# A two-layer encoder block: the Fourier projection unfolded, with its channels folded on eviction, and layer 1's weights split mostly in the down projection

## The chip, the cores and the metric

The kernel runs on one core of one Trainium2 chip. The metric is the device time of one execution in microseconds, as the median of several runs. Lower is better. One further execution was profiled; every row of the trace that is shown comes from that one.

## What is computed

A trunk of two layers over 512 positions and 1024 channels, all in float32. In each layer the Fourier part, the attention part and a convolutional feed-forward part (FFN) follow one another:

```python
h   = rmsnorm(x, norm1[l])
p   = h @ w_in[l]                       # columns: u (512) | q (8x64) | k (2x64) | v (2x64)
y_f = fft2(u, axes=(positions, channels), norm="ortho").real @ w_fourier[l] + b_fourier[l]
y_a = windowed_gqa(rope(rmsnorm(q)), rope(rmsnorm(k)), v, sink[l])   # |i-j| <= 128
x   = x + concat(rmsnorm(y_f), rmsnorm(y_a)) @ w_o[l]
h   = rmsnorm(x, norm2[l])
up  = dwconv3(h @ w_up[l])              # 1024 -> 2 x 2816
x   = x + (silu(up[:, :2816]) * up[:, 2816:]) @ w_down[l]
```

The real part of a two-dimensional FFT is cos·u·cos − sin·u·sin. Cosine rows are symmetric and sine rows antisymmetric, so each axis of length 512 can be folded: element i and element 512−i are added for the cosine half (indices 0 to 256) and subtracted for the sine half (255 values).

## The kernel before

**Numbers in two pieces.** Every operand of a large matmul is kept as a sum of two values, hi and lo, of a reduced-precision type. `split` and `wsplit` make them: ACT copies the value into hi (line 97 or 123), and DVE, or POOL where that is given, subtracts hi from the value to get lo (line 101 for a scaled source, through the helper `stt` on line 92; otherwise through the helper `tt` on line 89). `mm3` (lines 106 to 108) then issues three matmuls, hi·hi, lo·hi and hi·lo, into one PSUM bank. Since `act`, `tt` and `stt` are helpers, nearly all ACT work is on line 86 of the profile and most of DVE and POOL is on 89 and 92; the tiles tell the groups apart.

**Order of the work.** The kernel is written with a tile framework. It tracks the dependencies, gives out the buffers of each tag, and orders the instructions of each engine by a simulated timeline and by their place in the program, so the order on an engine isn't the order in the text. An engine takes its own instructions strictly in that order. Three things are set by hand: the number of buffers of each tag (`TEMPS`, `BANKS`), `issue_after` in `proj`, which holds the matmuls of the output projection's first half behind numbered steps of the attention, and the generator `presplit`.

**One layer, in the order of the program:**

1. `col_rstd` and `row_rstd` (lines 202 to 216) make the norm's factor `r1` per position down the partitions, and `rb1` along the rows. 
2. q, k and v: two groups (k with one q pair and v, then the other three q pairs), each 8 channel tiles × 4 position blocks × 3 matmuls of 384 columns. The positions are the stationary side (`xg`, tag `act`, 8 buffers).
3. `fold_h` (line 351): for each of the 8 channel tiles, h = x·g·rb1 on DVE, the positions folded (`fold`, line 299: a copy of two columns on DVE, an addition and a subtraction of 255 columns on POOL), and the result split into the tag `slab`.
4. `prep` (line 372) for k and q pair 3 (norm, rotary tables partly on POOL, split), then `turn_k` and `turn_q`, which transpose them on TensorE.
5. The Fourier projection (line 486): the weights' columns are folded too, by `load_wu` on DVE and POOL in layer 0. For each of 8 channel tiles, `mm3` runs on pieces `pee` (3 row pieces of 128, 128 and 1, 258 columns) and `poo` (2 row pieces, 256 columns): 8 × 5 × 3 = 120 matmuls.
6. `prep` for the q pairs 0 to 2, then `attention` for 4 pairs of heads: scores (line 450), a masked minimum on DVE (line 454), exponential on ACT, division on POOL (line 459), transposes on TensorE (line 462), split, and the product with v.
7. `stage_out` (line 515) evicts and splits `pee` and `poo`. Two DFT stages follow (line 526) of 36 matmuls each, against the tables `th` and `tl`, each with its eviction, then the projection with w_fourier (line 561), whose folded rows come in `w_fold` and are added on POOL in layer 0.
8. The output projection w_o in two halves (Fourier, attention), with the next norm's tiles made by `norm_tile` on the way.
9. The FFN in two halves of 11 tiles: 22 up projections (24 matmuls of 512 columns each) and 8 down projections (33 each).

**Layer 1's weights.** During layer 0's FFN `presplit(1)` loads layer 1's w_qkv, w_in, w_fold and w_o, splits them into `tA` tiles (6 buffers), and SyncE's queue stores the pieces in DRAM (`kept`, line 142); layer 1 fetches them with `fetch`. It makes 44 keys. `next(ahead)` makes one, and it stands after each up projection (line 658) and once after each half (line 692), so all are made during the up projections, one per 24 matmuls. Its raw loads use the ring `wraw` (3 buffers), which w_up and w_down use as well.

Of the kernel before, what the change touches and what calls it, by code (L numbers as in the profile page):

```python
# [37 lines left out]
def encoder_kernel(tc, t):  # L38
# [28 lines left out]
    def f(x):  # L67
# [4 lines left out]
    TEMPS = {"act": (1024, 8), "m4": (1024, 5), "slab": (1028, 4), "pT": (2560, 2),  # L72
             "tA": (512, 6), "tF": (512, 6), "sq": (512, 2)}
# [61 lines left out]
    def presplit(l):  # L135

        def keep(key, src):
# [4 lines left out]
            return lambda: [nc.sync.dma_start(o, f(z)) for o, z in zip(kept[key], two)]  # L142

        def store(waiting, w):
            if waiting:
                waiting.pop()()
            if w:
                waiting.append(w)

        late = []  # L150
        for grp in (1, 0):
            for kk in range(KT // 2):
                raw = wload(t["w_qkv"][l, grp, kk], 768)
                for i in range(2):
                    store(late, keep(f"qkv{grp}{2 * kk + i}", raw[:, i * 384:(i + 1) * 384]))
                    yield
        for kk in range(KT // 2):
            raw = wtile()
            nc.sync.dma_start(raw.rearrange("p (k c) -> p k c", k=2),
                              t["w_in"][l, 2 * kk * P:2 * (kk + 1) * P, 0:FW].rearrange("(k p) c -> p k c", p=P))  # L160
            for k in range(2):
                w = temp(512, "tA")
                fold(w, raw[:, k * 512:(k + 1) * 512], nc.vector)
                store(late, keep(f"u{2 * kk + k}", w))
                yield
        for j in range(NF):
            raw = wload(t["w_fold"][l, j], 1024)
            w = temp(512, "tA")
            tt(w[:, :256], raw[:, :256], raw[:, 512:768], ALU.add)
            tt(w[:, 256:], raw[:, 256:512], raw[:, 768:], ALU.subtract)  # L170
            store(late, keep(f"f{j}", w))
            yield
        for half in range(2):
            for mp in range(KT // 2):
                raw = wload(t["w_o"][l, half, :, mp * 1024:(mp + 1) * 1024], 1024)
                for i in range(2):
                    store(late, keep(f"o{half}{2 * mp + i}", raw[:, i * 512:(i + 1) * 512]))
                    yield
        store(late, None)
        while True:  # L180
            yield
# [65 lines left out]
    zero = temp(512, "sq")  # L247
    nc.vector.memset(zero, 0.0)
    warm = temp(512, "sq", F32R)
# [19 lines left out]
    def load_tables():  # L269
        for i in range(2):  # L270
            raw = wload(t["dft"][i], 512)
            th = cp.tile([P, 512], F32R, tag=f"th{i}", name=f"th{i}")
            tl = cp.tile([P, 512], F32R, tag=f"tl{i}", name=f"tl{i}")
            split(th, tl, raw)
            tab.append((th, tl))
        alt = wtile()[:1, :258]
# [4 lines left out]
    def add_square(acc, src, first, eng=nc.gpsimd, tag="sq"):  # L281
# [17 lines left out]
    def fold(dst, src, eng):  # L299

        nc.vector.tensor_copy(dst[..., 0:257:256], src[..., 0:257:256])
        tt(dst[..., 1:256], src[..., 1:256], src[..., 511:256:-1], ALU.add, eng)
        tt(dst[..., 257:512], src[..., 1:256], src[..., 511:256:-1], ALU.subtract, eng)

    def load_wu(l, kk):

        raw = wtile()
        nc.sync.dma_start(raw.rearrange("p (k c) -> p k c", k=2),
                          t["w_in"][l, 2 * kk * P:2 * (kk + 1) * P, 0:FW].rearrange("(k p) c -> p k c", p=P))
        out = []  # L310
        for k in range(2):
            w = temp(512, "tA")
            fold(w, raw[:, k * 512:(k + 1) * 512], nc.gpsimd)
            out.append(w)
        return out
# [4 lines left out]
    for l in range(L):  # L320

        r1 = col_rstd(acc, 1.0 / D)
        rb1 = row_rstd(r1)
        qraw = {}
        for grp in (1, 0):
            pq = [psum("mm" if b < 3 else "av") for b in range(NB)]
# [22 lines left out]
        hs = {}  # L349

        def fold_h(k, eng):
            hr = temp(512, "tF")
            hf = temp(512, "tF")
            stt(hr, x[k], g1[:, l, k:k + 1], rb1, ALU.mult, ALU.mult)
            fold(hf, hr, eng)
            hs[k] = pair("slab")
            split(hs[k][:, 0, :], hs[k][:, 1, :], hf)

        for k in range(4):
            fold_h(k, nc.gpsimd)  # L360
# [11 lines left out]
        def prep(us):  # L372
# [4 lines left out]
            for i, u in enumerate(us):  # L377
                two = temp(1024, "act").rearrange("p (z b h d) -> p z b h d", z=2, **dims)
# [99 lines left out]

        if l == 0:
            load_tables()  # L480

# [3 lines left out]

        pee = [psum(), psum(), psum("av")]
        poo = psum()
        for kk in range(KT // 2):
            if not l:
                wu = load_wu(l, kk)  # L490
            for k in (2 * kk, 2 * kk + 1):
                if k not in hs:
                    fold_h(k, nc.gpsimd)
                w = fetch(f"u{k}") if l else wsplit(wu[k % 2])
                h = hs[k]
                st, sp_ = k == 0, k == KT - 1
                we = [z[:, 0:258] for z in w]
                wo = [z[:, 256:512] for z in w]
                for m, (c0, c1) in enumerate(((0, 128), (128, 256), (256, 257))):
                    mm3(pee[m][:c1 - c0, :258], [h[:, s, c0:c1] for s in range(2)], we, st, sp_)  # L500
                mm3(poo[:, 0:256], [h[:, s, 257:385] for s in range(2)], wo, st, sp_, skip_group_check=True)
                mm3(poo[:127, 256:512], [h[:, s, 385:512] for s in range(2)], wo, False, sp_, skip_group_check=True)
# [7 lines left out]
        def tail_out(pe, scale):  # L510
            b = tp.tile([1, 2, 258], F32R, tag="tail", name=nm("tail"), bufs=2)
# [3 lines left out]
        def stage_out(pe, po, scale):  # L515
            tiles = []
            for m in range(2):
                a = pair("slab", 514)
                n = P - m
                split(a[:, 0, :258], a[:, 1, :258], pe[m][:, :258], scale=scale)  # L520
                split(a[:n, 0, 258:514], a[:n, 1, 258:514], po[:n, m * 256:(m + 1) * 256], scale=scale)
                tiles.append(a)
            return tiles, tail_out(pe, scale)

        ue, ut = stage_out(pee, poo, 1.0)
        for stage in range(2):
            pe = [psum() for _ in range(2)]
            po = psum()
            pe.append(psum())
            for m, (c0, c1) in enumerate(((0, 128), (128, 256), (256, 257))):  # L530
                o = pe[m][:c1 - c0, :258]
                for i in range(2):
                    u2 = [ue[i][:, s, :] for s in range(2)]
                    if stage == 0:
                        mm3(o, [z[:, c0:c1] for z in u2], [z[:, 0:258] for z in tab[i]], i == 0, False)
                    else:
                        mm3(o, [z[:, c0:c1] for z in tab[i]], [z[:, 0:258] for z in u2], i == 0, False)
# [244 lines left out]
```

## Time and profile before

| | |
|---|---|
| median of 3 runs | 1111.37 us (1110.5 to 1114.45) |
| the profiled execution, its own time | 1112.89 us |
| its span from first to last instruction | 1111.1 us |
| mean granted TensorE clock over the span | 0.988 |
| layer 0 up to the last matmul of the second norm | 0 to 227.1 us |
| layer 0's FFN | 226.9 to 573.2 us |
| layer 1 up to the same place | 579.8 to 766.1 us |
| layer 1's FFN | 765.9 to 1111.1 us |

In rows that group instructions, the columns are: line, engine, operation, output tile <- input tiles, shape, x count | busy time in us, mean ns of one | idle time of the engine just before them, and what ended it. In rows of windows: the window, its length, and for each engine busy us (x instructions), then the granted clock of TensorE (PEclk), the share of the DMA engines' time and GB/s. PE is TensorE's matmuls, PEld its weight loads. A matmul's duration overlaps its neighbours', so the pace of a dense stretch is read from the length of the stretch and the number of matmuls in it.

### The profile page before, as it was taken

To read this page: it belongs to the slowest core of one execution; us is meant where nothing else is said; L and a number is where in the kernel's file an instruction comes from. 1 tells how busy PE (TensorE), PEld (TensorE's weight loads), DVE (VectorE), ACT (ScalarE), POOL (GpSimd) and SP (SyncE) were. 2 spreads that over 40 slices of the span, in tenths; PEclk is the share of its full clock that TensorE was granted. 3 is DMA by queue.
4 is the path that set the end of the run, shared out by engine and by line. 5 is a ranking of instruction groups with operands and counts; after the bars stand their busy time and mean duration, and the time that the engine had idled before them with its cause. 6 is when DMAs were issued, how large, how long until landed. Compare 5 with 4: busy or idle time off the path is not lost.

```text
span 1111.1 us, 14836 instructions
## 1 busy us (share of the span) xinstructions
PE 1068.9 (96%) x5187; PEld 892.3 (80%) x5187; DVE 778.9 (70%) x1406; ACT 514.5 (46%) x964; POOL 278.1 (25%) x326
## 2 busy tenths in 40 slices
PE   7878899999999999999999899999999999999998
PEld 6776788788888888778889787878888888888887
DVE  8997874988883477887437968477878535787732
ACT  4536763565552244554412676245555323544421
POOL 5678654511010001111105344050201000010100
PEclk9978999999999999999999999999999999999999
DMA  6312113366643576763355510523232333333241
GB/s 218 110 58 95 39 39 119 122 215 229 207 147 93 196 249 232 231 218 105 87 168 174 188 58 20 171 76 95 95 97 82 104 97 97 112 89 101 78 130 59
DMA packets 58574, 141.65 MB, mean 127 GB/s; under 512 B 6521, under 2 KB 19074, under 8 KB 58498
## 3 DMA queue, kind: packets, MB, share of 16 engines
q1 hardware_dynamic: 58498, 140.69, 40.0%
q8 instruction: 41, 0.67, 0.2%
q14 instruction: 35, 0.29, 0.1%
HBM read 117.60 MB, written 23.07 MB: 127 GB/s over the span
## 4 chain that ended last, share of the span: by engine, by line
PE 72%; DVE 15%; DMA 6%; issue 3%; ACT 2%; POOL 1%; SPq 0%; DVEq 0%; POOLq 0%; ACTq 0%
PE ps L106 22%; PE ps L108 22%; PE ps L107 22%; DVE wlo L89 4%; DMA wraw<-in_w_o_dram 3%; DMA wraw<-in_w_fold_dram 2%; DVE tF L92 2%; DVE act L89 1%; DVE act L92 1%; PE ps L450 1%; PE ps L462 1%; DVE tA L89 1%; DVE tF L89 1%; DVE slab L89 1%; DMA wraw<-in_w_in_dram 1%
## 5 line engine op out<-in xcount | busy, mean ns | idle before, releaser
L89 DVE TENSOR_TENSOR wlo<-wraw,whi 128x512 fp32r<-128x512 f32 (+1 forms) x288 | 234.6, 816 | 113.8 <-ACT whi L86 111.8
L107 PE MATMUL ps<-act,wlo 128*128 128x512 f32 x768 | 300.4, 392 | 3.7 <-DVE wlo L89 3.6
L108 PE MATMUL ps<-act,whi 128*128 128x512 f32 x768 | 300.2, 391 | 3.2 <-DVE act L92 3.1
L86 ACT ACTIVATE whi<-wraw 128x512 fp32r<-128x512 f32 (+1 forms) x300 | 183.5, 613 | 256.1 <-PE ps L108 231.7
L106 PE MATMUL ps<-act,whi 128*128 128x512 f32 x768 | 299.7, 390 | 0.0
L89 POOL TENSOR_TENSOR tF<-tF,tF 128x512 f32<-128x512 f32 x44 | 61.0, 1387 | 535.9 <-DVE tF L92 492.4
L107 PEld LDWEIGHTS ps<-act,wlo 128*128 128x128 f32 x768 | 144.6, 188 | 36.2 <-DVE wlo L89 6.2
L108 PEld LDWEIGHTS ps<-act,whi 128*128 128x128 f32 x768 | 144.6, 188 | 35.5 <-DVE act L92 6.1
L106 PEld LDWEIGHTS ps<-act,whi 128*128 128x128 f32 x768 | 144.5, 188 | 30.2
L92 DVE SCALAR_TENSOR_TENSOR tF<-tF,pb,tF 128x511 f32<-128x511 f32 x176 | 132.8, 759 | 8.7 <-ACT tF L86 5.5
L89 DVE TENSOR_TENSOR tF<-ps,rb 128x512 f32<-128x512 f32 x104 | 70.6, 686 | 43.8 <-PE ps L108 32.6
L106 PE MATMUL ps<-slab,whi 128*128 128x512 f32 (+2 forms) x228 | 87.3, 383 | 1.0 <-ACT slab L86 1.0
L107 PE MATMUL ps<-slab,wlo 128*128 128x512 f32 (+2 forms) x228 | 85.2, 374 | 0.0
L108 PE MATMUL ps<-slab,whi 128*128 128x512 f32 (+2 forms) x228 | 84.9, 375 | 0.1
L86 ACT ACTIVATE tF<-tF,pb 128x512 f32<-128x512 f32 x88 | 71.5, 815 | 15.7 <-DVE tF L89 12.3
L89 DVE TENSOR_TENSOR x<-x,ps 128x512 f32<-128x512 f32 (+1 forms) x49 | 33.0, 676 | 46.1 <-PE ps L108 46.1
L89 POOL TENSOR_TENSOR acc<-acc,sq 128x512 f32<-128x512 f32 x28 | 43.0, 1535 | 60.0 <-ACT sq L86 59.3
L107 PE MATMUL ps<-pT,wlo 128*128 128x512 f32 (+1 forms) x132 | 51.0, 386 | 0.0
L108 PE MATMUL ps<-pT,whi 128*128 128x512 f32 (+1 forms) x132 | 50.8, 385 | 0.0
L106 PE MATMUL ps<-pT,whi 128*128 128x512 f32 (+1 forms) x132 | 50.8, 385 | 0.0
L106 PEld LDWEIGHTS ps<-slab,whi 128*128 128x128 f32 x228 | 42.9, 188 | 8.8 <-ACT slab L86 1.4
L108 PEld LDWEIGHTS ps<-slab,whi 128*128 128x128 f32 x228 | 42.8, 188 | 8.5 <-DVE slab L89 0.4
(171 smaller groups left out, 1791.3 us busy)
## 6 DMA issues: line engine op xcount, KB each, us to landing
wraw<-in_w_up_dram SPq DMA_DIRECT2D x88, 512.0 KB, 3.8
wraw<-in_w_down_dram SPq DMA_DIRECT2D x32, 512.0 KB, 3.5
kept<-tA SPq DMA_DIRECT2D x56, 256.0 KB, 4.3
wraw<-in_w_o_dram SPq DMA_DIRECT2D x16, 512.0 KB, 3.6
whi<-kept SPq DMA_DIRECT2D x28, 256.0 KB, 3.5
wlo<-kept SPq DMA_DIRECT2D x28, 256.0 KB, 3.7
wraw<-in_w_qkv_dram SPq DMA_DIRECT2D x16, 384.0 KB, 3.5
kept<-tA SPq DMA_DIRECT2D x32, 192.0 KB, 2.1
```

The costliest lines, as they stand in the source:

```text
L86: return nc.scalar.activation(out, in_, func, **kw)
L89: return (eng or nc.vector).tensor_tensor(out, a, b, op=op)
L92: return nc.vector.scalar_tensor_tensor(out=out, in0=a, scalar=s, in1=b, op0=op0, op1=op1)
L106: nc.tensor.matmul(out, a[0], b[0], start=start, stop=False, **kw)
L107: nc.tensor.matmul(out, a[1], b[0], start=False, stop=False, **kw)
L108: nc.tensor.matmul(out, a[0], b[1], start=False, stop=stop, **kw)
L450: nc.tensor.matmul(sc[:, :n], qT[p][:, e, i * P:(i + 1) * P], kT[g][:, s, j0 * P:(j1 + 1) * P], start=s == 0, stop=s == 1)
L462: tr = nc.tensor.transpose(pp[:, j * P:(j + 1) * P], pr[:, j * P:(j + 1) * P], ident)
```

## The change

The Fourier projection takes the same stationary tiles `xg` as q, k and v, and the unfolded weights. The result comes out with positions down the partitions and 512 channels along the columns, one PSUM bank for each of the 4 position blocks. On eviction it is scaled by `r1` and its channels are folded. `fold_h`, `rb1` and the folding of w_in are gone. The position axis is no longer folded before the first DFT stage: that stage contracts over 4 blocks of 128 positions, with two more table tiles, made from the first two by alternating signs on ACT. It now stands in front of `prep`.

```diff
 TEMPS:  "slab" (1028, 4) -> (1024, 4);  "tA" (512, 6) -> (512, 5);  "sq" (512, 2) is gone (its users take "tF")
-        rb1 = row_rstd(r1)
-            pq = [psum("mm" if b < 3 else "av") for b in range(NB)]
+            pq = [psum(("mm", "mm", "mm", "av")[b] if grp else ("sc", "sc", "tp", "tp")[b]) for b in range(NB)]
...
-        def fold_h(k, eng):
...
-        for k in range(4):
-            fold_h(k, nc.gpsimd)
+        if l == 0:
+            load_tables()
+        pu = [psum("mm" if b < 3 else "av") for b in range(NB)]
+        for kk in range(KT // 2):
+            raw = None if l else load_wu(l, kk)
+            for k in (2 * kk, 2 * kk + 1):
+                w = fetch(f"u{k}") if l else wsplit(raw[:, (k % 2) * 512:(k % 2 + 1) * 512])
+                for b in range(NB):
+                    mm3(pu[b], [xg[k][:, s, b * P:(b + 1) * P] for s in range(2)], w, k == 0, k == KT - 1)
+        ub = []
+        for b in range(NB):
+            uf = temp(512, "tF")
+            fold(uf, pu[b], r1[:, b:b + 1])
+            a = pair("act")
+            split(a[:, 0, :], a[:, 1, :], uf)
+            ub.append(a)
...
+    def fold(dst, src, scale):
+        up = temp(256, "tF")
+        act(up[:, :255], src[:, 257:512], scale=scale)
+        nc.vector.tensor_scalar(dst[:, 0:257:256], src[:, 0:257:256], scale, None, op0=ALU.mult)
+        stt(dst[:, 1:256], src[:, 1:256], scale, up[:, 254::-1], ALU.mult, ALU.add)
+        stt(dst[:, 257:512], src[:, 1:256], scale, up[:, 254::-1], ALU.mult, ALU.subtract)
...
-                two = temp(1024, "act")...          # in prep
+                two = temp(1024, "slab")...
...
-        pee = [psum(), psum(), psum("av")]          # the folded projection, 120 matmuls
...
+        for m, (c0, c1) in enumerate(((0, 128), (128, 256), (256, 257))):      # first DFT stage
+            for b in range(NB):
+                mm3(pe[m][:c1 - c0, :258], [ub[b][:, s, c0:c1] for s in range(2)], [z[:, 0:258] for z in tab[b]],
+                    b == 0, b == NB - 1)
+        for m in range(2):
+            for b in range(NB):
+                mm3(po[:, m * 256:(m + 1) * 256], [ub[b][:, s, 256 + m * P:384 + m * P] for s in range(2)],
+                    [z[:, 256:512] for z in tab[b]], m == 0 and b == 0, b == NB - 1, skip_group_check=True)
```

The second stage keeps its 36 matmuls. The folded rows of w_fourier are now loaded without the part that repeats (`load_wf`: 2 × 256 of 1024 columns), and `fold_w` makes sum and difference on DVE. `wsplit` of them in layer 0 is on DVE and no longer on POOL, and the squares of the Fourier output are added up on DVE.

`presplit` becomes a list of jobs. The raw tile comes from the tag `m4` (5 buffers), no longer from `wraw`, and it is loaded one job ahead:

```diff
         def keep(key, src):
             two = [temp(n, "tA", F32R) for _ in range(2)]
             split(two[0], two[1], src)
...
+            store()
+            late.append(lambda: [nc.sync.dma_start(o, f(z)) for o, z in zip(kept[key], two)])
...
+        got = jobs[0][0]()
+        for n, (_, keys) in enumerate(jobs):
+            for i, key in enumerate(keys):
+                keep(key, fold_w(got[i]) if key[0] == "f" else got[i])
+                if i == len(keys) - 1 and n + 1 < len(jobs):
+                    got = jobs[n + 1][0]()
+                yield
...
-                    next(ahead)                       # after each up projection
+                    if (2 * n + z) % 3 == 2:
+                        next(ahead)
...
-                tt(ys_[0], ys_[0], ys_[1], ALU.mult, nc.gpsimd)
+                tt(ys_[0], ys_[0], ys_[1], ALU.mult, nc.gpsimd if l else nc.vector)
...
             for m in range(KT):                       # down projection
+                next(ahead)
+                next(ahead)
```

That is 7 keys in the up projections of a half and 16 in its down projections. The key's `u` jobs no longer fold.

More of the change, by code (lines that the diff above doesn't have):

```diff
@@ L141, in keep, with store @@
             kept[key] = [dp.tile([P, n], F32, tag=f"{key}{s}", name=nm("kept")) for s in range(2)]
[L142 to L150, printed above, removed]
+            store()
+            late.append(lambda: [nc.sync.dma_start(o, f(z)) for o, z in zip(kept[key], two)])
+        def store():
+            while late:
+                late.pop()()
@@ L161, in presplit @@
[L161 to L165, printed above, removed]
-        for j in range(NF):
[L167 to L172, printed above, removed]
+            jobs.append((lambda kk=kk: wu(kk), [f"u{2 * kk + i}" for i in range(2)]))
@@ new lines, in encoder_kernel @@
+        ue, ut = stage_out(pe, po, 1.0)
+        pe = [psum(), psum()]
+        po = psum()
+        pe.append(psum())
+        for m, (c0, c1) in enumerate(((0, 128), (128, 256), (256, 257))):
+            o = pe[m][:c1 - c0, :258]
+            for i in range(2):
+                mm3(o, [z[:, c0:c1] for z in tab[i]], [ue[i][:, s, 0:258] for s in range(2)], i == 0, False)
+            for s in range(2):
+                nc.tensor.matmul(o, altr[:, c0:c1], ut[:, s, :], start=False, stop=s == 1)
@@ L691, in encoder_kernel @@
                     nxt.append(norm_tile(m, g1[:, l + 1, :], acc))
-            next(ahead)
             xg = nxt
```

178 lines of the change are left out of this document (70 added, 108 removed).

## The prediction

> **What bounds the kernel now.** I read the page first, for the engines and the slices, then the windows by stage, then the groups of instructions in the one window that looked wrong, then the waits.
>
> ```profile
> PE 1068.9 (96%) x5187; PEld 892.3 (80%) x5187; DVE 778.9 (70%) x1406; ACT 514.5 (46%) x964; POOL 278.1 (25%) x326
> ...
> PE   7878899999999999999999899999999999999998
> ...
> PEclk9978999999999999999999999999999999999999
> ```
>
> TensorE carries the span. Added columns cost time wherever PE is at 9, and a gain must come from the few slices where it isn't: the second to fifth, where PEclk dips too, one near the middle of layer 0's FFN, and around the norms. The windows put sizes on them (layer 0's stretch from 32 to 90; dense FFN; layer 0's and layer 1's FFN; dense folded projection; dense q projection; attention and output part of layer 0 and layer 1).
>
> ```profile
> 32.00:90.00 58.00, 44.95 (x251) 39.01 (x249) 55.48 (x95) 24.71 (x50) 44.38 (x51) 0.83 0.25 75
> 800.00:900.00 100.00, 100.00 (x439) 82.21 (x438) 66.60 (x88) 42.23 (x64) 9.03 (x7) 1.00 0.31 93
> 226.00:573.00 347.00, 343.32 (x1501) 280.47 (x1501) 239.45 (x371) 162.23 (x267) 41.99 (x34) 1.00 0.57 181
> 766.00:1100.00 334.00, 334.00 (x1465) 274.51 (x1464) 218.84 (x292) 141.41 (x214) 28.79 (x22) 1.00 0.32 97
> 624.00:629.20 5.20, 5.20 (x46) 4.88 (x45) 4.54 (x6) 0.37 (x1) 4.57 (x5) 1.00 0.79 244
> 594.00:604.00 10.00, 9.96 (x58) 9.64 (x57) 9.90 (x16) 2.43 (x4) 7.16 (x9) 1.00 0.23 63
> 82.00:178.00 96.00, 87.74 (x529) 73.92 (x530) 71.52 (x207) 64.46 (x164) 61.93 (x92) 0.96 0.17 56
> 630.00:717.00 87.00, 83.72 (x507) 70.44 (x508) 61.74 (x198) 52.38 (x144) 28.51 (x64) 1.00 0.24 78
> ```
>
> These rows give the pace of a matmul at full clock. 512 columns: 100/439 = 0.228 us. 384 columns: 10/58 = 0.172, say 0.174, since one record in the count began earlier. 256 or 258 columns: records there last about 0.28 us, so those counted began within 5.48 us, and 5.48/46 = 0.119.
>
> In 32 to 90 DVE is busy 55.5 of 58 us and POOL 44.4, while PE stands idle for 13 us and runs at a mean clock of 0.83. DVE sets that stretch.
>
> **What fills DVE there, and what goes.** Groups of DVE, POOL and PE in that window, and then two DVE groups in layer 1 (606 to 717), where POOL is mostly idle:
>
> ```profile
> L92 DVE SCALAR_TENSOR_TENSOR tF<-x,pa,rb 128x512 f32<-128x512 f32 x8 | 8.6, 1079 | 0.1
> L89 DVE TENSOR_TENSOR slab<-tF,slab 128x512 fp32r<-128x512 f32 x8 | 7.6, 975 | 0.0
> L89 DVE TENSOR_TENSOR wlo<-tA,whi 128x512 fp32r<-128x512 f32 x8 | 7.1, 887 | 0.0
> L301 DVE COPY tF<-tF 128x2 f32<-128x2 f32 x8 | 4.0, 496 | 0.0
> L301 DVE COPY tA<-wraw 128x2 f32<-128x2 f32 x8 | 3.1, 425 | 0.0
> L92 DVE SCALAR_TENSOR_TENSOR slab<-ps,slab 128x258 fp32r<-128x258 f32 (+2 forms) x6 | 2.3, 410 | 0.1
> L92 DVE SCALAR_TENSOR_TENSOR qk2q<-qk2q,qk2v 128x16 f32<-128x16 f32 x3 | 1.8, 594 | 0.0
> L89 POOL TENSOR_TENSOR tF<-tF 128x255 f32<-128x255 f32 x16 | 15.1, 966 | 14.8 <-DVE tF L92 14.8
> L89 POOL TENSOR_TENSOR tA<-wraw 128x255 f32<-128x255 f32 x16 | 14.3, 923 | 0.5 <-DMA wraw<-in_w_in_dram 0.5
> L107 PE MATMUL ps<-whi,slab 128*128 128x258 f32 (+3 forms) x40 | 12.9, 354 | 3.6 <-DVE slab L89 3.6
> L108 PE MATMUL ps<-wlo,act 128*128 128x384 f32 x31 | 10.6, 346 | 1.3 <-DVE wlo L89 1.3
> ```
> ```profile
> L89 DVE TENSOR_TENSOR slab<-tF,slab 128x512 fp32r<-128x512 f32 x8 | 5.3, 684 | 0.1
> L92 DVE SCALAR_TENSOR_TENSOR qk2q<-qk2q,qk2v 128x16 f32<-128x16 f32 x3 | 0.5, 176 | 0.1
> ```
>
> (Of ACT, for below:)
>
> ```profile
> L86 ACT ACTIVATE slab<-tF 128x512 fp32r<-128x512 f32 x8 | 4.9, 622 | 7.6 <-PE ps L108 4.5 <-POOL tF L89 2.1 <-POOL wraw L89 1.0
> L86 ACT ACTIVATE slab<-ps 128x258 fp32r<-128x258 f32 (+2 forms) x6 | 2.2, 381 | 12.6 <-PE ps L108 10.8 <-PE ps L540 1.5 <-DVE slab L92 0.3
> ```
>
> The change takes `fold_h` and the weight fold out: on DVE 8.6 + 7.6 + 4.0 + 3.1 = 23.3 us, on POOL 15.1 + 14.3 = 29.4 of its 44.4 us. The second effect is as large as it is hidden: a DVE instruction of 16 columns takes 594 ns here and 176 in layer 1, and a 512-column subtraction 975 against 684, because POOL is working beside them. With POOL two thirds empty, the 24 small steps of the two q and k norms, of which the group shown is the slowest, shrink by about half of its 0.42 us on the mean, 24 × 0.2 = 5 us, and the 8 weight splits by 8 × 0.2 = 1.6 us.
>
> New on DVE are four folds on eviction. From the rows: a step of about 256 columns out of PSUM costs 0.41 us, with two of them per block, the two-column scaling lies between 0.18 and 0.5 (I take 0.2), and the subtraction for lo is 0.68. That is 4 × 1.7 = 6.8 us. DVE's load becomes 55.5 − 23.3 − 6.6 + 6.8 = 32 us.
>
> **Part 1, layer 0 from 32 to 90.** PE's own work now, at the paces above: 91 matmuls of 384 columns (the shown 31 and two groups of 30), 15.8 us; 120 of the folded projection, 14.3; the 40 others (transposes and first DFT matmuls) at about 0.115, 4.6. Sum 34.7 us in 58. The change makes the 120 matmuls into 8 × 4 × 3 = 96 of 512 columns, 96 × 0.228 = 21.9, so +7.6. The first DFT stage has (3 + 2) × 4 × 3 = 60 matmuls for 36: 24 × 0.119 = +2.9. `row_rstd` of `rb1` goes; this piece of the chain has its price:
>
> ```profile
> 586.96 0.89 PE ps L213 x8
> ```
>
> So PE has 9.6 us more per layer, and 44.3 us here. With DVE at 32 us, PE becomes the bound, and the projection needs nothing from the q and k preparation, so it covers it: 22 us of matmuls, in which DVE has 5.6 us of weight splits to do. I take 46 us for the stretch, 1.7 above PE's work, for the first folds. **−12.0 us.** The end at 44.3 is one bound, −13.7. The other is that the chain fold, split, DFT isn't covered: one block's fold in sequence (ACT 0.4 and 0.6, DVE 1.7) four times is 11 us at worst, −2.7. I stay near the first, because the transposes of k and q and the first scores are ready by then and need no `ub`.
>
> **Part 2, layer 0's attention and output.** Between 82 and 178 PE is idle for 8.3 us, in layer 1's same part (630 to 717) for 3.3. The difference, 5, is DVE's lateness and POOL's rotary work; I take back 1.5, since the folded w_fourier rows come to DVE: 8 additions of 256 columns and 4 splits, 8 × 0.41 + 4 × 0.69 = 6 us, less one `stage_out` of 4 × 0.41 plus the tail. **−1.5 us.**
>
> **Part 3, layer 1.** No cold clock here. PE waits, from the waits of TensorE between 586 and 640:
>
> ```profile
> PE ps L414 <- DVE m L89: 2.3, 1, 2.3
> PE ps L106 <- DVE vz L92: 1.1, 1, 1.1
> PE ps L425 <- ACT m L86: 0.6, 1, 0.6
> ```
>
> All three wait for preparation on ACT or DVE that would now lie under 22 us of projection matmuls: −4.0, and with a few tenths of fetch waits −4.5. The added 9.6 stays. **+5.1 us.** The bounds are +9.6 (nothing recovered) and +4.
>
> **Part 4, layer 0's FFN.** 1501 matmuls in 347 us, at layer 1's pace (334/1465 = 0.228) 342.2: 4.8 us are lost, 3.7 of them idle. The waits between 370 and 500 and one piece of the chain show the reason:
>
> ```profile
> ACT tA L86 <- DMA wraw<-in_w_o_dram: 19.0, 8, 3.2
> DVE tA L89 <- DMA wraw<-in_w_fold_dram: 9.9, 4, 3.4
> ```
> ```profile
> 377.00 5.59 DMA wraw<-in_w_fold_dram
> ```
>
> ACT and DVE stand in front of a raw tile that was loaded just before it is used, because `wraw` is shared with w_up; the FFN's own splits queue behind on the same engine. With rows of their own and a job's lead, the load is hidden by the preceding job. The keys move to the down projections, where each output has 33 × 0.228 = 7.5 us of matmuls. Costs of DVE per output there, from the groups of the whole run and the DMA issues:
>
> ```profile
> L89 DVE TENSOR_TENSOR wlo<-wraw,whi 128x512 fp32r<-128x512 f32 x240 | 200.2, 834 | 79.3 <-ACT whi L86 77.7
> L89 DVE TENSOR_TENSOR x<-x,ps 128x512 f32<-128x512 f32 x47 | 32.2, 687 | 39.4 <-PE ps L108 39.4
> L92 DVE SCALAR_TENSOR_TENSOR act<-x,pa,act 128x512 fp32r<-128x512 f32 x32 | 32.1, 1008 | 4.1 <-ACT act L86 3.7
> kept<-tA SPq DMA_DIRECT2D x56, 256.0 KB, 4.3
> ```
>
> Three weight splits 2.5, the addition 0.7, two keys 1.4, and in the second half the norm 1.0: 5.6 us at most, under 7.5. The gated product that comes from POOL to DVE (22 × 0.69 us) falls in the up projections, which lose two thirds of their keys. **−4.5 us.** Bounds: −4.8, and above zero for the first rival.
>
> **Sum.** −12.0 − 1.5 + 5.1 − 4.5 = −12.9. The profiled execution took 1112.89 us (1111.1 of span and 1.8 around it), so 1100.0; it lies 1.5 above the median of the runs shown, 1111.37, so I forecast 1098.5. A measurement of this kernel tells about 0.5% from no change: 5.6 us, so faster is below 1105.8 and slower above 1116.9.
>
> **A rule against it.** PE's clock after a wait, in two windows: the wait for `slab`, and what came behind it.
>
> ```profile
> 67.60:71.20 3.60, 0.04 (x1) 0.00 (x0) 3.60 (x7) 1.84 (x4) 2.81 (x3) 0.92 0.21 85
> 71.20:77.80 6.60, 6.56 (x32) 6.01 (x33) 6.50 (x12) 0.00 (x0) 5.28 (x8) 0.53 0.00 0
> ```
>
> A wait of 3.6 us was followed by 6.6 us at 0.53 of the clock, which cost 6.6 × 0.47 = 3.1 us more. The Trainium skill ("TensorE: Matmul & The Clock Gate", part 1, the clock gate) has the clock halved after one idle window of about 3.4 us and full again after one busy window of that length. By that rule an uncovered fold would cost its wait and about 1.7 us; the trace says nearly twice that. The rows decide, and it enters one rival.
>
> **Rivals.**
> *Stores stall the down projections (slower).* Each key takes two of now five `tA` buffers, two keys come back to back, and a store lands 4.3 us after its issue. A key's stores are issued only after the next key's split, and the key after that already needs one of its buffers. If DVE stands for one landing per output, 5.6 + 4.3 = 9.9 us against 7.5, with 2.4 lost, and without the norm 1.4: 8 × 2.4 + 8 × 1.4 = 30 us. It decides once the stall exceeds 1.9 us in the second half. The time: 1098.5 + 4.5 + 30 − 4 (banks that run ahead) = 1129. Against it: the keys of one output and of the next lie 7.5 us apart, longer than a landing, and DVE's order can put the FFN's own splits first.
> *The wait moves (no change).* The folds aren't covered, in both layers: 11 − 1.7 = 9 us in layer 0, some 5 in layer 1, and 3.1 of cold clock after the first: 1098.5 + 17 = 1115. For it: all four banks finish together, at the last channel tile, and ACT has its own queue of evictions.
> *TensorE packs closer (faster still).* DVE freed in both layers lets attention start earlier; PE's idle time of 3.3 us in layer 1's attention and 5 us in layer 0's goes too, with some switching loss: 1098.5 − 10 = 1088.
> That the change does nothing can be excluded: the matmul counts differ.
>
> **Chances.** Forecast 0.57 (1092 to 1105, with a tenth of it above the line), packing 0.15, moved wait 0.18 (a third of it each way of the lines, mostly inside), stores 0.10. Faster: 0.52 + 0.15 = 0.67. The same: 0.05 + 0.11 = 0.16. Slower: 0.10 + 0.07 = 0.17. The range runs from 1088 to 1115: it takes in the packing and most of the moved wait and leaves out the stores.
>
> **What would show it.** In the changed profile, 96 matmuls of 512 columns from `act` directly behind the q projection, without idle time over 1 us; PEclk at 1.0 from 32 to 90; the small DVE steps of `qk2q` under 250 ns; layer 0's output projection done some 13 us earlier than now; layer 1 from its first norm to the second 5 us longer; layer 0's FFN within 343 us with no wait for a raw tile. I am wrong if PE waits over 3 us for `ub`, if DVE waits for `kept` in the down projections, or if layer 1 grows by over 10 us.

## The result, and the profile after

The changed kernel took 1129.91 us (median of 4 runs, 1129.04 to 1130.74) and the kernel before 1112.05 beside it. The ratio is 1.0159, 95% interval 1.0137 to 1.018: slower by 1.6%, where 1098.5 was forecast and the range ended at 1115. The profiled execution took 1129.04 us, with a span of 1127.3 and a mean granted clock of 0.976.

The page of the kernel after, in the lines shown of before:

```profile
PE 1083.1 (96%) x5171; PEld 915.4 (81%) x5171; DVE 749.2 (66%) x1396; ACT 520.5 (46%) x960; POOL 177.8 (16%) x239
...
PE   8989869999999999999999997799999999999998
...
PEclk9989969999999999999999998799999999999999
```

A slice is 28.2 us. DVE and POOL lost 30 and 100 us of work, as the change says, and the weak slice 23 of before (611 to 639 us, in layer 1) is full. But PE has new holes: slice 6 (141 to 169 us) and slices 25 and 26 (676 to 733), all with a low clock. They lie where the two layers have attention and the first half of w_o. The windows of the kernel after show how deep they are:

```profile
32.00:90.00 58.00, 53.00 (x301) 48.04 (x300) 49.07 (x116) 33.64 (x75) 16.94 (x19) 0.94 0.30 98
231.80:573.20 341.40, 341.40 (x1512) 282.82 (x1511) 242.41 (x371) 168.77 (x265) 9.54 (x11) 1.00 0.53 177
130.00:190.00 60.00, 46.58 (x205) 39.29 (x203) 29.77 (x81) 23.16 (x49) 16.29 (x16) 0.80 0.27 88
651.00:741.00 90.00, 75.71 (x411) 64.84 (x410) 50.60 (x170) 39.44 (x108) 20.03 (x52) 0.89 0.21 65
```

The kernel before, in the same stages (in layer 1 its attention and the first half of w_o are over at 717):

```profile
130.00:190.00 60.00, 57.48 (x319) 49.32 (x320) 38.42 (x116) 33.62 (x82) 29.54 (x47) 1.00 0.18 54
651.00:717.00 66.00, 64.94 (x377) 54.62 (x377) 45.27 (x144) 35.96 (x98) 21.53 (x49) 1.00 0.28 88
```

From 130 to 190 the changed kernel issues 205 matmuls for 319, at a clock of 0.80 for 1.00, and no other engine is near full. Nothing is saturated: something waits. Split at the first matmul of layer 1's q, k and v (573.1 us before; the 579.8 of the earlier table is the norm's matmuls, which come a little later):

| us | layer 0 | layer 1 | span |
|---|---|---|---|
| before | 573.1 | 538.0 | 1111.1 |
| forecast (−18.0, +5.1) | 555.1 | 543.1 | 1098.2 |
| after | 573.2 | 554.1 | 1127.3 |

So layer 0's whole gain is missing, and layer 1 lost 16 instead of 5. TensorE's waits of the kernel after between 60 and 240 us (total, times, longest):

```profile
PE ps L106 <- ACT act L86: 5.0, 1, 5.0
PE ps L106 <- ACT tF L86: 4.3, 1, 4.3
PE ps L208 <- DVE accF L89: 3.7, 1, 3.7
PE ps L496 <- DVE pT L89: 3.3, 4, 1.9
PE ps L215 <- DVE nr L92: 2.5, 1, 2.5
```

The first is the wait for `ub`, the first DFT stage's operand. The second, third and fifth are a chain: Fourier output, its squares, its norm. Before, this chain lay among attention's steps. ScalarE's timeline shows when it starts (start, us, engine, line, operation, out <- in). The kernel before:

```profile
107.25 0.48 ACT L86 ACTIVATE tF<-ps,pa 128x258 f32<-128x258 f32 x1 [0.59 <-PE ps L108]
...
121.38 0.46 ACT L86 ACTIVATE tF<-ps,pa 128x258 f32<-128x258 f32 x1
...
129.00 0.69 ACT L86 ACTIVATE act<-ps,pa 128x512 fp32r<-128x512 f32 x1
```

The kernel after:

```profile
121.51 0.59 ACT L86 ACTIVATE tF<-ps 128x512 f32<-128x512 f32 x1
...
140.82 0.67 ACT L86 ACTIVATE act<-ps,pa 128x512 fp32r<-128x512 f32 x1
...
143.76 0.58 ACT L86 ACTIVATE tF<-ps 128x512 f32<-128x512 f32 x1
144.24 0.47 ACT L86 ACTIVATE tF<-ps,pa 128x258 f32<-128x258 f32 x1
```

`tF<-ps,pa` of 258 columns is the eviction of one Fourier output tile (`u`), `act<-ps,pa` closes a pair of heads, and `tF<-ps` is the square of that pair's output. Before, all four evictions were done before the first pair closed. After, the first one comes right behind the last pair's square, at 144 us. With the norm behind it, the first 96 matmuls of w_o, which would fill attention's pauses, all run in one piece behind it (before, they are spread from 140 to 178 us):

```profile
167.00:190.00 23.00, 22.70 (x96) 18.17 (x97) 8.45 (x14) 6.34 (x12) 8.98 (x7) 0.99 0.24 69
```

### The profile page after: what moved, and what is told of

It reads as the page before. It is cut to its first block, busy times and chain, and to the rows that moved or that the text cites. A ratio compares the mean times of both kernels' runs of the same rounds, so it can differ in the third digit from the quotient of the medians.

```text
span 1127.3 us, 14774 instructions
## 1 busy us (share of the span) xinstructions
PE 1083.1 (96%) x5171; PEld 915.4 (81%) x5171; DVE 749.2 (66%) x1396; ACT 520.5 (46%) x960; POOL 177.8 (16%) x239
## 4 chain that ended last, share of the span: by engine, by line
PE 87%; DVE 6%; ACT 2%; issue 2%; DMA 1%; POOL 1%; SPq 0%; DVEq 0%; ACTq 0%
PE ps L106 28%; PE ps L108 28%; PE ps L107 27%; PE ps L484 1%; DVE tA L488 1%; PE ps L496 1%; PE ps L208 1%; DVE wlo L89 1%; DVE pT L89 1%; ACT tA L86 1%; DVE act L92 1%; DMA kept<-tA 1%; DVE tF L92 1%; PE ps L215 1%; DVE x L89 1%
## 5 line engine op out<-in xcount | busy, mean ns | idle before, releaser
L86 ACT ACTIVATE whi<-wraw 128x512 fp32r<-128x512 f32 (+1 forms) x308 | 189.2, 617 | 315.3 <-PE ps L108 278.5
L89 DVE TENSOR_TENSOR wlo<-wraw,whi 128x512 fp32r<-128x512 f32 (+1 forms) x300 | 228.3, 762 | 90.6 <-ACT whi L86 88.8
L106 PE MATMUL ps<-slab,whi 128*128 128x512 f32 (+2 forms) x228 | 88.4, 389 | 7.9 <-ACT tF L86 6.8
L89 POOL TENSOR_TENSOR acc<-acc,tF 128x512 f32<-128x512 f32 x28 | 39.7, 1417 | 352.2 <-ACT tF L86 350.3
L108 PE MATMUL ps<-slab,whi 128*128 128x512 f32 (+2 forms) x228 | 87.0, 384 | 0.3 <-DVE slab L89 0.3
L89 POOL TENSOR_TENSOR tF<-tF,tF 128x512 f32<-128x512 f32 x22 | 30.5, 1386 | 270.4 <-DVE tF L92 229.2
L108 PE MATMUL ps<-wlo,act 128*128 128x384 f32 (+1 forms) x192 | 68.2, 358 | 1.5 <-DVE wlo L89 1.5
L107 PE MATMUL ps<-whi,act 128*128 128x384 f32 (+1 forms) x192 | 68.8, 358 | 0.8 <-DVE act L92 0.8
L106 PE MATMUL ps<-whi,act 128*128 128x384 f32 (+1 forms) x192 | 67.9, 356 | 0.0
L106 PEld LDWEIGHTS ps<-slab,whi 128*128 128x128 f32 x228 | 45.4, 199 | 17.3 <-ACT tF L86 7.2
L108 PEld LDWEIGHTS ps<-slab,whi 128*128 128x128 f32 x228 | 45.3, 199 | 8.8 <-DVE slab L89 1.2
```

The costliest lines, as they stand in the source:

```text
L86: return nc.scalar.activation(out, in_, func, **kw)
L89: return (eng or nc.vector).tensor_tensor(out, a, b, op=op)
L106: nc.tensor.matmul(out, a[0], b[0], start=start, stop=False, **kw)
L107: nc.tensor.matmul(out, a[1], b[0], start=False, stop=False, **kw)
L108: nc.tensor.matmul(out, a[0], b[1], start=False, stop=stop, **kw)
```

## The experiments

**Theory A**: the tag `sq` is gone and its users take `tF`, so attention's squares and the Fourier output now draw on one tag. The framework gives a tag's tiles out in the order of the program's text, and attention stands first there, so the Fourier output must wait until attention has taken its last tile. **The rivals** in the expectations look elsewhere. B is the added TensorE work and the later first DFT stage, which would make the Fourier chain late whatever the tags; C is the count, too few `tF` tiles for all their users. The kernel before took 1112.05 to 1113.47 us (median) beside these runs. All kernels compute the whole reference.

| run | us | ratio to before, 95% interval |
|---|---|---|
| after, squares on `tA` | 1110.18 | 0.998 (0.9966 to 0.9995) |
| before, squares on `tF` | 1150.28 | 1.0336 (1.0312 to 1.036) |
| before, new spread of the split alone | 1108.39 | 0.9958 (0.994 to 0.9976) |
| after, 5 `tF` and 1 `sq` | 1096.95 | 0.9849 (0.9819 to 0.988) |
| before, 8 `tF`, no `sq` | 1152.6 | 1.0343 (1.0325 to 1.0362) |
| 5 + 1, rows on GpSimd | 1095.71 | 0.9842 (0.982 to 0.9864) |
| 5 + 1, rows held back | 1087.36 | 0.9761 (0.9745 to 0.9777) |
| after, attention later in the text | 1094.46 | 0.9826 (0.9806 to 0.9846) |
| after, attention later and rows held back | 1084.15 | 0.9725 (0.9701 to 0.9749) |
| rows held back, old spread of the split | 1087.97 | 0.9766 (0.9742 to 0.979) |
| before, squares on `tF`, attention later | 1113.19 | 0.9991 (0.9974 to 1.0009) |
| the 1084.15 version, `slab` of 1028 | 1090.02 | 0.9792 (0.9774 to 0.981) |

### Which tag the squares use

In the changed kernel, another tag for attention's squares:

```diff
-    add_square(accA, ...)                 # the helper's default tag, here "tF"
+    add_square(accA, ..., tag="tA")
```

> The changed kernel with one edit: the squares of the attention output take a tile of the tag tA and no longer one of tF. Theory A (tiles of one tag are given out in the program's order, so the Fourier output's eviction, which asks for a tF tile later in the program than the attention's squares, had to wait for the last pair of heads, and w_o's first half lost its cover): the Fourier output is evicted among the attention steps, the idle stretches around 130 to 167 and 684 to 718 us shrink by 25 to 33 us together, 1097 to 1105 us. Theory B (the extra TensorE work and the later first DFT stage leave the Fourier chain too late whatever the buffers): 1122 us or more. Theory C (too few tF tiles, their count and not their order): 1122 or more, since tF keeps 6 tiles with three users fewer; a gain of at most 5.

It took 1110.18, 20 less than the changed kernel, where theory A had 25 to 33. The mechanism holds and the price is off; `tA` also holds attention's probabilities, which may be why, but no run shows it. TensorE's waits between 60 and 240 us are now

```profile
PE ps L106 <- ACT act L86: 4.9, 1, 4.9
PE ps L484 <- DVE nmax L488: 4.4, 4, 2.0
```

and the chain of the Fourier output is gone from them. Line 484 is the scores, which wait for the masked minimum on DVE.

The reverse, in the kernel before: its one edit gives it the shared tag and leaves all else.

```diff
-    add_square(accA, ...)                 # the helper's default tag, here "sq"
+    add_square(accA, ..., tag="tF")
```

> The kernel before with that one edit alone the other way: the squares of the attention output take tF tiles in place of their own tag. Nothing else is changed. Theory A: slower by 15 to 30 us, 1127 to 1142, with the Fourier output's evictions after the last pair of heads and w_o's first half in one uncovered piece. Theory B: within 3 us of 1112, since its TensorE work is that of before. Theory C: within 5 us.

1150.28: the shared tag alone costs this kernel 37 us, more than expected. That speaks against theory B, since this kernel has none of the added TensorE work. In the changed kernel, a tile of its own for the squares, taken from `tF`:

```diff
-    "tF": (512, 6)
+    "tF": (512, 5), "sq": (512, 1)
...
-    add_square(accA, ...)
+    add_square(accA, ..., tag="sq")
```

> The changed kernel with one tF tile fewer (5) and that tile as a tag of its own for the squares of the attention output. The total number of tiles is that of the changed kernel. Theory A: the order of giving out is what matters, so about as fast as with the squares on tA, 1097 to 1108 us. Theory C (the number of tF tiles): slower than the changed kernel, over 1130.

1096.95: 33 us less than the changed kernel, with fewer `tF` tiles and the same bytes. That speaks against the count. From 130 to 190 us PE is full again:

```profile
130.00:190.00 60.00, 58.70 (x302) 49.08 (x302) 42.11 (x96) 32.85 (x74) 31.62 (x37) 1.00 0.36 118
```

### Order or number of the tiles

The kernel before with more `tF` tiles and all of its bytes:

```diff
-    "tF": (512, 6), "sq": (512, 2)
+    "tF": (512, 8)
...
-    def add_square(acc, src, first, eng=nc.gpsimd, tag="sq"):
+    def add_square(acc, src, first, eng=nc.gpsimd, tag="tF"):
```

So the squares of the two norms of x are on `tF` here too, and not only attention's.

> The kernel before with its two `sq` tiles made into two more `tF` tiles (8 tF, no sq); everything else as before, so the fold of h and of the weights stays on VectorE. Theory A (tiles of one tag are given out in program order, so the Fourier output's evictions wait for the last of attention's squares, however many tiles there are as long as they are fewer than attention's 16 squares): 1135 to 1155, near the 1150.28 that the shared tag gave with six tiles; the w_o matmuls of the first half stand in one piece behind attention. Theory C (too few tiles, not their order): with as many bytes as before the time is back at 1112 plus or minus 6.

1152.6, as with six tiles. (The expectation's figure of 16 attention squares is wrong: the trace has three that need a tile in a layer.) Eight tiles would hold those three and the first Fourier tiles side by side, and still ScalarE's timeline has the Fourier output behind the last square:

```profile
154.34 0.60 ACT L86 ACTIVATE tF<-ps 128x512 f32<-128x512 f32 x1 [0.82 <-DVE act L92]
154.84 0.84 ACT L86 ACTIVATE tF<-ps,pa 128x258 f32<-128x258 f32 x2
```

So it is the order. If the order is that of the text, moving the text must be enough. The changed kernel with six shared tiles and three lines moved:

```diff
-        attention(3, True)
-        for p in range(3):
-            attention(p, False)
...
             yf.append(y)
+        attention(3, True)
+        for p in range(3):
+            attention(p, False)
         rbF = row_rstd(...)
```

> The changed kernel with its one tag of six `tF` tiles, but with the calls of attention moved behind the Fourier output in the program's text; the issue order by cost stays the scheduler's. Theory A (order of the tag's tiles by program text): the Fourier output's evictions now hold their tiles before attention's squares, overlap is back, 1094 to 1110, with the w_o matmuls spread over attention. If it isn't the order of the tiles but their count, 1122 or more, as the changed kernel's 1129.9. A risk under theory A: now attention's first squares wait for the Fourier output's tiles, and with them attention's probabilities; then 1105 to 1120.

1094.46, 35 us less than the changed kernel, without a byte or an instruction more. In ScalarE's timeline the squares now stand behind the Fourier output:

```profile
103.64 0.48 ACT L86 ACTIVATE tF<-ps,pa 128x258 f32<-128x258 f32 x1 [0.18 <-PE ps L108]
...
118.37 0.48 ACT L86 ACTIVATE tF<-ps,pa 128x258 f32<-128x258 f32 x1 [0.69 <-PE ps L108]
...
129.82 0.60 ACT L86 ACTIVATE tF<-ps 128x512 f32<-128x512 f32 x1
```

The same three lines moved in the kernel before with its squares on `tF`:

> The kernel before with attention's squares on the shared tag `tF` (1150.28 with attention first in the text) and the calls of attention moved behind the Fourier output. Theory A (the tag's tiles are given out in program order): the 38 us go, 1104 to 1118. If the shared tag costs by its number of tiles or in another way, 1130 or more.

1113.19, from 1150.28: level with the kernel before. Theory A is shown from both sides: the shared tag costs 37 us in the kernel before and 33 to 35 in the changed one, and the order of the text takes it away in both. Neither does it alone: with a tag of their own for the squares, attention can stand first in the text at no such cost (1112 and 1096.95).

### The split's spread alone

The kernel before with the new job list, its tiles and its place in the down projections, and none of the projection's change:

```diff
+                if i == len(keys) - 1 and n + 1 < len(jobs):
+                    got = jobs[n + 1][0]()
...
-                    next(ahead)
+                    if (2 * (fi - f0) + z) % 3 == 2:
+                        next(ahead)
...
+                next(ahead)
+                next(ahead)
```

> The kernel before with the new splitting of layer 1's weights alone (raw tiles from m4, one job ahead, 7 keys in the up and 16 in the down projections of a half; u and f keys still folded on DVE). Forecast: layer 0's FFN 4 to 6 us shorter, 1106 to 1108 us. The rival of the prediction (stores stall the down projections): 1120 or more.

1108.39, a ratio of 0.9958: at the slow edge of the forecast, and with no stall. Its FFN of layer 0 takes 342.4 us, from 347.0, without a gap on PE:

```profile
227.50:569.90 342.40, 342.40 (x1506) 282.04 (x1505) 254.52 (x369) 167.61 (x264) 38.71 (x34) 1.00 0.53 180
```

That window opens at the norm's last matmuls, and how many of the FFN's matmuls come before these differs from kernel to kernel. A stretch of equal work is the last 1056 matmuls, from the first down projection of the first half to layer 1: 247.3 us before, 241.7 here, 239.4 in the changed kernel. The run changes the raw tiles' lead and the place of the keys at once, and doesn't tell which of them is worth the 5.5 us.

In the changed kernel the waits of DVE and ACT in the FFN of layer 0 (231 to 574) show what the store rival had feared, and that it doesn't reach PE, which has not one wait there:

```profile
DVE tA L89 <- DMA kept<-tA: 7.4, 4, 3.1
```
```profile
ACT tA L86 <- DMA m<-in_w_o_dram: 8.7, 5, 3.0
```

Is the new spread still worth it where the folds are gone? The version with the rows held back (below), with the old spread (its raw tiles come from `wraw` again):

```diff
...
-                    if (2 * n + z) % 3 == 2:
-                        next(ahead)
+                    next(ahead)
...
-                next(ahead)
-                next(ahead)
...
```

> The version with the rows held back (1087.36) with layer 1's weights split as in the kernel before: one step behind each tile of the gate stage, none in the down projections, the stores one step later, the raw rows in the tile `wraw`. The new spread alone took 3.7 to 4.6 us off the kernel before. If it is worth as much here: 1091 to 1093. If the folds that are gone from the split (eight folded input-weight tiles less) made the old spread harmless: 1087 to 1089.

1087.97 against 1087.36, intervals on top of each other; those 1056 matmuls take 240.3 us, against 239.4. So the spread and the rest of the change in this FFN lead to the same few us and don't add. That rest is two things which no run separates: the folds of w_in are out of the split, and the gated product is on DVE and no longer on POOL.

### The wait of 5 us behind the projection

ScalarE's timeline in the kernel after, before that wait ends at 74.5 us:

```profile
67.81 0.63 ACT L86 ACTIVATE whi<-wraw 128x512 fp32r<-128x512 f32 x1 [6.85 <-DVE wraw L338]
71.57 0.63 ACT L86 ACTIVATE whi<-wraw 128x512 fp32r<-128x512 f32 x1 [3.12 <-DVE wraw L338]
72.10 1.18 ACT L86 ACTIVATE tF<-ps,nr 128x255 f32<-128x255 f32 x3
```

`tF<-ps,nr` is the fold's eviction of the projection. In the run with the rows held back (below) ScalarE takes the first at 67.04 us, so that its bank was ready then; but ScalarE takes its instructions in order, and ahead of it stand high copies of w_fourier rows, each waiting for `fold_w` on DVE (line 338). First, in the five-plus-one version, these folds and low halves on GpSimd:

```diff
-            w = ... wsplit(fold_w(load_wf(l, j)))
+            w = ... wsplit(fold_w(load_wf(l, j), nc.gpsimd), nc.gpsimd)
```

> The five-plus-one version (1096.95) with layer 0's fold of the w_fourier rows and their low halves on GpSimd instead of VectorE. The wait of 5 us for `act` behind the projection is put down to ScalarE, which holds the four high copies of these rows, each waiting for VectorE's fold, ahead of the projection's evictions. If VectorE's queue is what makes these copies late, the wait shrinks to 1 to 3 us and the time is 1093 to 1096. If GpSimd is as late with them as VectorE was (it is slower on such tiles), 1097 to 1100. If the copies aren't the cause, the wait stays at 5 us and the time at 1097.

The wait went from 5.2 to 4.3 us and the time by 1.2, inside the intervals: neither of the first two cases, and inconclusive by itself. Then the rows behind the folds:

```diff
-            split(a[:, 0, :], a[:, 1, :], uf)
+            hi = act(a[:, 0, :], uf)
+            lo = tt(a[:, 1, :], uf, f(a[:, 0, :]), ALU.subtract)
...
-            w = fetch(f"f{j}") if l else wsplit(fold_w(load_wf(l, j)))
+            if l:
+                w = fetch(f"f{j}")
+            else:
+                with tc.issue_after(hi.ins), tc.issue_after(lo.ins):
+                    w = wsplit(fold_w(load_wf(l, j)))
```

> The five-plus-one version (1096.95) with layer 0's fold and split of the w_fourier rows put behind the last fold's eviction in the order of ScalarE and VectorE. If the four high copies ahead of the evictions make the wait of 5 us and the cold clock behind it (7.3 us lost from 68.8 to 80 us), both go: TensorE goes from the projection to the second DFT stage in under 1.5 us, the granted clock stays at 1.0 from 60 to 80 us, and the time is 1089 to 1092. If the evictions themselves are what is late, the wait stays and the time is 1097 or more, since the rows now come later.

1087.36, 9.6 less, a little more than expected. ScalarE takes the first eviction at 67.04 us, and the window from 60 to 80 loses its hole. The five-plus-one version:

```profile
60.00:80.00 20.00, 14.84 (x75) 12.67 (x74) 19.70 (x37) 8.11 (x16) 11.19 (x11) 0.83 0.41 132
```

With the rows held back:

```profile
60.00:80.00 20.00, 19.62 (x122) 16.41 (x122) 18.25 (x41) 11.29 (x24) 7.84 (x8) 1.00 0.10 27
```

Both cures together (attention later in the text, rows held back):

> Six `tF` tiles with attention's calls later in the text (1094.46), and the rows of w_fourier held back as in the run that did this (1096.95 to 1087.36, 9.6 less). If the two gains are of different stretches (the fold at 60 to 80 us, attention from 100 us on), they add: 1085, 1083 to 1088. If the later rows now delay what attention covers, 1088 to 1094.

1084.15, ratio 0.9725 (0.9701 to 0.9749): the gains add, and this beats both kernels. Its page:

```profile
PE 1064.2 (98%) x5171; PEld 899.1 (83%) x5171; DVE 753.2 (70%) x1396; ACT 517.1 (48%) x960; POOL 184.6 (17%) x239
...
PEclk9999999999999999999999999999999999999999
```

### One number: the columns of `slab`

The matmuls of the same FFN code in layer 1 followed each other 0.7% closer in every kernel that had `slab` at 1024 columns. The best version with only this:

```diff
-    "slab": (1024, 4)
+    "slab": (1028, 4)
```

> The best version (1084.15) with one number changed: the tag `slab` gets back its 1028 columns (tiles of 1028 instead of 1024 values; no instruction and no order changes). In every kernel so far with 1028 the first 400 matmuls behind the last norm take 90.8 us and the 400 after them, down projections whose moving side lies in `slab`, 92.0; in every kernel with 1024 both take 90.7 to 90.8. If the place of the `slab` tiles sets this pace, the second 400 take 92.0 again and the time is 1088 to 1090 (2.2 us for each of the two FFNs by these kernels, and up to 1 for the output projections). If the pace comes with the fold of h or anything else that those kernels share, it stays at 90.8 and the time at 1084.

1090.02 (ratio 0.9792, 0.9774 to 0.981, against 0.9725), spans 1087.3 and 1082.7: 4.6 us more by the spans, 5.9 by the medians. The second 400 matmuls behind the last norm take 91.9 us and not 90.7. Groups of TensorE between 860 and 925 us, with mean ns behind the comma. With 1024:

```profile
L106 PE MATMUL ps<-act,whi 128*128 128x512 f32 x38 | 14.8, 389 | 0.0
...
L106 PE MATMUL ps<-slab,whi 128*128 128x512 f32 x20 | 7.8, 389 | 0.0
L106 PE MATMUL ps<-m,whi 128*128 128x512 f32 x18 | 7.0, 389 | 0.0
```

With 1028:

```profile
L106 PE MATMUL ps<-act,whi 128*128 128x512 f32 x33 | 12.8, 389 | 0.0
...
L106 PE MATMUL ps<-slab,whi 128*128 128x512 f32 x20 | 7.9, 393 | 0.0
L106 PE MATMUL ps<-m,whi 128*128 128x512 f32 x18 | 7.1, 395 | 0.0
```

The tiles `m` are those of the tag `m4`, whose size is the same in both. They are slowed as well, and so are those of `pT`.

## Why the prediction was wrong

**The step that failed** is none of the four prices but an entry that has none. The change says that `sq` is gone and that its users take `tF`; the prediction gave this no price and no sentence, as if a tag were only storage. Parts 2 and 3 (−1.5 and +5.1) can only hold if attention is still covered by the w_o matmuls of the Fourier half, and that isn't said there. The runs put 33 to 35 us on that entry. Without it the same change takes 1094.46 or 1096.95 (ratios 0.9826 and 0.9849), which is on the forecast's side and close to its 1098.5. How close is partly luck: the rows of w_fourier cost 9.6 us that no part has, and against that stand some 5 us for the columns of `slab`, a second entry of the change without a price, and another 4 to 5 us by which layer 1 does better than part 3.

Here are the four parts as differences from the kernel before, by places that hold about the same work in each kernel. The first row ends with the 251st matmul from 32 us on (90.8 us before; the prediction has as many matmuls on both sides). The second ends with the first down projection of layer 0, so that it holds the first half's up projections too.

| us | forecast | after | attention later | and rows held back |
|---|---|---|---|---|
| part 1, from 32 us | −12.0 | −6.4 | −5.6 | −13.2 |
| part 2, attention, output, first up projections | −1.5 | +14.4 | −3.1 | −5.4 |
| part 4, the last 1056 matmuls of layer 0 | −4.5 | −7.9 | −7.9 | −7.9 |
| part 3, layer 1 | +5.1 | +16.0 | −1.9 | −1.9 |

- *The reading of the page*: the weak slice that it puts near the middle of layer 0's FFN is slice 23, 611 to 639 us, in layer 1. No price rests on it.
- *The bound of 32 to 90 and the small steps*: right. The projection's 96 matmuls follow the q projection from 46.7 to 68.7 us without idle time, and the small DVE steps shrank as said. In the window 32 to 90 of the kernel after:

```profile
L92 DVE SCALAR_TENSOR_TENSOR qk2q<-qk2q,qk2v 128x16 f32<-128x16 f32 x3 | 0.5, 175 | 0.1
```

- *Part 1, −12.0*: right in size only once the rows of w_fourier are out of the way. The prediction put the folded w_fourier rows into part 2, as DVE time. They also stand in ScalarE's order ahead of the folds, and there they cost 9.6 us. This is its second rival (the moved wait) in layer 0 only; layer 1 fetches these rows ready made and has no such wait. Its own mark, a wait over 3 us for `ub`, came true at 5.0, and the clock from 32 to 90 was 0.94 where 1.0 was forecast.
- *Part 2, −1.5*: fell with the shared tag. With both causes removed, the whole of layer 0 gains 26.5 us for the forecast 18.0.
- *Part 3, +5.1*: measured +16.0 with the shared tag, past the 10 that the prediction names as a mark of being wrong, but −1.9 without. Of those 7 us under the forecast, some 2 to 3 are the pace that comes with `slab`. The rest lies ahead of the down projections; the third rival (closer packing) would have it there, and no run took it apart.
- *Part 4, −4.5*: right in direction and near in size: −5.5 for the spread alone over equal work, and 341.4 us for the FFN (forecast 343 at most). In the changed kernel the spread is worth only 1.0 us, and 2.4 of the 7.9 us are the pace that comes with `slab` (241.7 with 1028 columns and 239.4 with 1024 in the last run's pair). Two of its marks failed without harm: DVE does wait for `kept` and ACT for raw tiles, but not PE.
- *The store rival* (slower, 1129) has the right time by accident: PE has no wait in that FFN, and the spread alone is faster.
- *The clock rule*: the windows of the kernel after, the wait for `ub` and what follows it:

```profile
69.50:74.50 5.00, 0.06 (x1) 0.00 (x0) 4.77 (x13) 2.87 (x7) 0.84 (x2) 0.76 0.81 264
74.50:78.00 3.50, 3.45 (x14) 3.09 (x15) 3.50 (x9) 3.24 (x7) 3.50 (x4) 0.50 0.49 184
78.00:81.50 3.50, 3.50 (x29) 3.17 (x28) 2.48 (x4) 2.07 (x5) 0.14 (x1) 0.87 0.02 5
```

 After 5.0 us of waiting, 3.5 us run at 0.50 and 3.5 at 0.87: 3.5 × 0.50 + 3.5 × 0.13 = 2.2 us lost; the kernel before showed 3.1. In both kernels the granted clock was at half for 6.8 us, from 70.6 to 77.4 before and from 72.1 to 78.9 after; the loss differs because the wait ended 0.6 us into that stretch before and 2.4 us into it after. By one busy window of the Trainium skill ("TensorE: Matmul & The Clock Gate", part 1) the estimate is 1.7, and both traces are above it. The Trainium skill also says there that the window runs freely, and the two rows would fit that, but no run here moved a wait within it.

What stays open: why the squares on `tA` cost 13 us more than on a tile of their own (the scores' wait for DVE is seen, its cause isn't tried), whether moving attention in the text is better than a tile of their own for the squares (with the rows held back, 1084.15 and 1087.36 have touching intervals), and why a shared tag follows the text even with tiles to spare: the runs show that it does, not how the framework decides it.

## What to carry to other kernels

A tag is an order as well as a store: when a change lets two chains share a tag, read which of them stands first in the text, and price the other as waiting for it. The same holds for an in-order engine: list what the change puts ahead of each eviction, not only how long it takes. And when a stage turns slow with no engine full, look for the instruction that starts right behind an unrelated one.

## What the hardware showed beyond that

One number of one tag, with no instruction changed, sets the pace of a whole stage. With tiles of `slab` of 1028 values of four bytes, matmuls of 512 columns in the down projections show 392 to 393 ns from `slab`, 392 to 396 from `m` and 390 to 394 from `pT`; with 1024 all show 389. Those from `act` show 389 in both. Since `m4` and `pT` kept their size, it can't be the size of the tile alone that a matmul reads; that the place of the tiles in memory moved with it is a guess, and which places are slow wasn't tried. All six kernels with 1028 take 91.9 to 92.0 us for the second 400 matmuls behind the last norm, and all eight with 1024 take 90.7. Over the kernel that is 4.6 to 5.9 us, a quarter to a third of the changed kernel's gain once its order is mended (17 to 19 us).
